# One-hots for the spreading of expert weights: from VectorE alone to GpSimd and VectorE, one turn earlier

## The chip, the cores and the metric

The kernel runs on one core of one Trainium2 chip. The metric is the device time of one execution in microseconds; the kernel before takes 3607.58 us, the median of three runs (3606.92 to 3616.43).

## The reference

Two networks are computed one after the other on 256 tokens of width 1024, in float32. The first has two layers of mixed attention and a dense feed-forward part; the change does not touch it. The second has two layers of attention, each followed by a feed-forward part with 16384 experts of which every token uses few. For a block of tokens, cut to what matters:

```python
q = (hb @ w_q).reshape(n, PEER_HEADS, PEER_QDIM)              # 8 heads
s1, s2 = q1 . sub_keys[0], q2 . sub_keys[1]                   # 128 keys each
v1, i1 = lax.top_k(s1, 16);  v2, i2 = lax.top_k(s2, 16)
top_s, pos = lax.top_k(v1 + v2 for all 16 x 16 pairs, 16)
expert = i1 * 128 + i2 at pos                                 # 8 x 16 = 128 per token
g = jax.nn.softmax(top_s, axis=-1)
act = gelu(sum_d u_tab[expert] * hb)
out = sum_hk (g * act) * v_tab[expert]
```

In layer 0 this is done for the 256 tokens and for 256 tokens of a context; in layer 1 only for the 256 tokens.

## The kernel before, in words

The kernel gathers no rows of the tables. It computes every one of the 128 x 128 experts for every token and multiplies each activation with a weight that is zero where the token did not choose the expert. An expert group e is the 128 experts with the same second index.

`ahead` walks the groups e = 0 to 127 (0 to 125 in layer 1). For each, `hidden` loads 512 KB of the table u, splits it into a high and a low part (`cut_in_two`, then `split`: ScalarE casts, L198, VectorE subtracts, L199; the tile tag "ws" has four buffers, two pairs), multiplies it on TensorE with the tokens in three products (`mac`, L232 to L234; 24 matmuls of 256 columns for 256 tokens, 48 for 512), applies the gelu on ScalarE (L1104) and stores the result in HBM (`kept`). 256 tokens of a group are called a unit here. In layer 0 the context half of the first 39 groups has been stored before, so layer 0 has 39 + 2 x 89 = 217 units and layer 1 has 126. `experts` then reads everything back, multiplies with the weights (tensor G) and with the table v.

While `ahead` runs, side generators are advanced after each unit. A plan (P0 for layer 0, P1 for layer 1) gives each a unit at which it starts and a rate in steps per unit. There are two kinds. `choose` finds a block's 16 best per head on VectorE and ends with R, which holds for every token (column) and every one of its 128 choices (partition) the first index, the second index, and the weight g in two parts. `spread` turns R of one block of 128 tokens into the dense weights of these tokens for all 128 x 128 experts, and writes them to G. Layer 0 has four blocks, two for the tokens and two for the context; layer 1 has two. In P0 the spreads start at units 38, 83, 121 and 169 with rates 0.9, 0.8, 0.9 and 0.95; in P1 at 45 and 85 with rates 0.5 and 0.85, so that the two overlap. In layer 0 a generator that loads rows of ada_w into buffers of the tag "wb" (`ada_rest`, VectorE L766) starts with the last spread.

One step of `spread` handles four tokens, and is called a turn here; a spread has 32. For each token VectorE makes three one-hot matrices of 128 choices by 128 keys in f16, in one tile E of the tag "wb" (three buffers): the first index compared with 0 to 127 (L1056), and the second index compared and multiplied by either part of g (L1058, twice). TensorE multiplies the first, as the stationary operand, with each of the other two (L1061), into a PSUM tile of four tokens; ScalarE copies that to a tile of 16 tokens (L1062), which goes to HBM once full (L1064). The four tokens' matmuls follow the one-hots of the same turn in the program. A planner of the language orders the instructions of each engine and adds the semaphores, so that pieces of a turn can stand between pieces of other work; each engine then runs its instructions in that order.

Of the kernel before, what the change touches and what calls it, by code (L numbers as in the profile page):

```python
# [12 lines left out]
F16 = mybir.dt.float16  # L13
U32 = mybir.dt.uint32
AF = mybir.ActivationFunctionType
ALU = mybir.AluOpType
AX = mybir.AxisListType

P = 128
# [5 lines left out]
NT = 16  # L25
GSCALE = 2.0 ** 14
# [27 lines left out]
class Net:  # L54
# [72 lines left out]
    def more_consts(self):  # L127
        nc, io = self.nc, self.io
        self.iota = self.const("iota", [P, P])
        self.mask_q = self.const("mask_q", [P, P])  # L130
        self.mask_k = self.const("mask_k", [P, P])
        self.mask_c = self.const("mask_c", [P, 2, 15])
        self.valid = self.const("valid", [P, 2])
        self.rope1 = self.const("rope1", [P, 2, 2, 8])
        self.rope2 = self.const("rope2", [P, 2, 2, P])
        self.iota16 = self.cst.tile([P, P], F16, tag="iota16", name="iota16")
        nc.vector.tensor_copy(self.iota16, self.iota)
        self.ones4 = self.cst.tile([4, S], F32, tag="ones4", name="ones4")
        nc.vector.memset(self.ones4, 1.0)
        self.cone = self.cst.tile([P, 1], F32, tag="cone", name="cone")  # L140
        nc.vector.memset(self.cone, 1.0)
# [821 lines left out]
    def choose(self, sd, s):  # L963


        nc = self.nc
        room = self.t(sd.t8, [P, 2048])

        def cut(a, n, k, dtype=F32):
            r = room[:, a:a + n]  # L970
            return (r if dtype is F32 else r.bitcast(dtype)).rearrange("p (h k) -> p h k", k=k)

        v, iu, fi = cut(0, 256, 16), cut(256, 256, 16, U32), cut(512, 128, 16, F16)
        ts, pu = cut(768, 128, 16), cut(896, 128, 16, U32)
        pi, pf = cut(1024, 128, 16, U32), cut(1152, 128, 16)
        sel = room[:, 1280:1664].rearrange("p (c h k) -> p c h k", c=3, k=16)
        gz = room[:, 1664:1672]
        ra, rb = cut(1672, 128, 16), cut(1800, 128, 16)
        for hh in range(16):
            tmp = self.t("k2", [P, P])  # L980
            self.top16(v[:, hh], iu[:, hh], s[:, hh], tmp)
            yield
        nc.vector.tensor_copy(fi, iu)
        cand = self.t(sd.t8, [P, 8, 112])
        v4 = v.rearrange("p (h c) k -> p h c k", c=2)
        for lo, n, a0, m in ((0, 4, 0, 16), (64, 12, 4, 4)):
            nc.vector.tensor_tensor(cand[:, :, lo:lo + n * m].rearrange("p h (a b) -> p h a b", b=m),
                                    v4[:, :, 0, a0:a0 + n, None].to_broadcast([P, 8, n, m]),
                                    v4[:, :, 1, None, 0:m].to_broadcast([P, 8, n, m]), op=ALU.add)
        yield  # L990
        for h in range(8):
            tmp = self.t("k2", [P, 112])
            self.top16(ts[:, h], pu[:, h], cand[:, h], tmp)
            yield

        far = pf
        nc.vector.tensor_copy(far, pu)
        nc.vector.tensor_scalar(far, far, 63.5, None, ALU.is_gt)
        for half in range(2):
            for r, (sh, mask) in ((ra, (4, 15)), (rb, (2, 3))):  # L1000
                if half == 0:
                    nc.vector.tensor_scalar(pi, pu, sh, None, ALU.logical_shift_right)
                else:
                    nc.vector.tensor_scalar(pi, pu, mask, None, ALU.bitwise_and)
                nc.vector.tensor_copy(r, pi)
            yield
            if half == 0:
                nc.vector.tensor_scalar(rb, rb, -12.0, None, ALU.add)
            nc.vector.tensor_sub(rb, rb, ra)
            nc.vector.tensor_mul(rb, rb, far)  # L1010
            nc.vector.tensor_add(ra, ra, rb)
            f4 = fi.rearrange("p (h c) k -> p h c k", c=2)
            yield
            for k in range(0, 16, 8):
                eq = self.t("k2", [P, 8, 8, 16], F16)
                nc.vector.tensor_tensor(eq, ra[:, :, k:k + 8, None].rearrange("p h k r -> p k h r").to_broadcast([P, 8, 8, 16]),
                                        self.iota[:, None, None, 0:16].to_broadcast([P, 8, 8, 16]), op=ALU.is_equal)
                yield
                nc.vector.tensor_mul(eq, eq, f4[:, None, :, half].to_broadcast([P, 8, 8, 16]))
                yield  # L1020
                for n in (8, 4, 2):
                    nc.vector.tensor_add(eq[:, :, :, 0:n], eq[:, :, :, 0:n], eq[:, :, :, n:2 * n])
                nc.vector.tensor_add(sel[:, half, :, k:k + 8].rearrange("p h k -> p k h"), eq[:, :, :, 0], eq[:, :, :, 1])
                yield
        gs = sel[:, 2]
        nc.vector.tensor_sub(gs, ts, ts[:, :, 0:1].to_broadcast([P, 8, 16]))
        nc.scalar.activation(gs, gs, AF.Exp)
        nc.vector.tensor_reduce(gz, gs, AX.X, ALU.add)
        nc.vector.reciprocal(gz, gz)
        nc.vector.tensor_mul(gs, gs, gz[:, :, None].to_broadcast([P, 8, 16]))  # L1030
        pt = self.p(sd.pt, [P, 3, P])
        for j in range(3):
            nc.tensor.transpose(pt[:, j], sel[:, j].rearrange("p h k -> p (h k)"), self.ident)
        R = self.t("R", [P, 4, P], bufs=2)
        g = self.t("k2", [P, P])
        g16 = self.t("k2", [P, P], F16)
        nc.scalar.copy(R[:, 0:2], pt[:, 0:2])
        nc.scalar.activation(g, pt[:, 2], AF.Copy, scale=GSCALE)
        nc.vector.tensor_copy(g16, g)
        nc.vector.tensor_copy(R[:, 2], g16)  # L1040
        nc.vector.tensor_sub(R[:, 3], g, R[:, 2])
        return R

    def spread(self, r, Gd, nb):


        nc = self.nc
        for q in range(P // NT):
            st = self.t("k8", [P, P, NT])
            for m in range(0, NT, 4):  # L1050
                n = q * NT + m
                pG = self.p("C", [P, 4, P])
                E = self.t("wb", [P, 4, 3, P], F16)
                for j in range(4):
                    k0, k1, g0, g1 = (r[:, i, n + j:n + j + 1] for i in range(4))
                    nc.vector.tensor_scalar(E[:, j, 0], self.iota16, k0, None, ALU.is_equal)  # L1056
                    for i, g in enumerate((g0, g1)):
                        nc.vector.tensor_scalar(E[:, j, 1 + i], self.iota16, k1, g, ALU.is_equal, ALU.mult)  # L1058
                for j in range(4):
                    for i in range(2):  # L1060
                        nc.tensor.matmul(pG[:, j], E[:, j, 0], E[:, j, 1 + i], start=i == 0, stop=i == 1)  # L1061
                nc.scalar.activation(st[:, :, m:m + 4], pG.rearrange("p n e -> p e n"), AF.Copy, scale=1 / GSCALE)  # L1062
                if m == NT - 4:
                    nc.sync.dma_start(Gd[:, nb + q], st)  # L1064
                yield

    def routing(self, l, hs, Gd, order, early, plan):

        ss = [self.t("k8", [P, 16, P]) for _ in range(2 * len(hs))]
        R = {}

        def choose(i):
            R[i] = yield from self.choose(self.rt, ss[i])

        def spread(gen, i, nb):
            self.done(gen)
            yield from self.spread(R[i], Gd, nb)

        gens = [choose(i) for i, _ in order]
        for _ in self.key_scores(l, hs, ss):
            for g in gens[:early]:
                next(g), next(g)
        gens += [spread(g, *o) for g, o in zip(gens, order)]
        return [(t, g, r) for g, (t, r) in zip(gens, plan)]
# [324 lines left out]
```

## Time and profile before

| | |
|---|---|
| median of three runs | 3607.58 us (3606.92 to 3616.43) |
| profiled execution | 3616.49 us, span 3614.7 us |
| TensorE matmul busy | 3506.5 us (97%), 22400 matmuls |
| weight load busy | 3053.3 us (84%) |
| VectorE busy | 2563.6 us (71%), 6767 instructions |
| ScalarE busy | 1520.0 us (42%) |
| GpSimd busy | 51.9 us (1%), 72 instructions |
| mean granted TensorE clock | 0.991 of full speed |
| chain of work that ended last | 67% TensorE, 21% VectorE, 8% DMA; L1058 6%, L1056 2%, L199 4% |

The profile is of one execution. Busy time is the time in which at least one instruction of an engine runs; matmuls are pipelined, so they overlap one another, and TensorE can be busy throughout and still do more or less work in a microsecond. The instructions of VectorE overlap a little too: the next starts before the one in front of it has ended, so the distance from start to start is what an instruction takes of the engine.

### The profile page before, as it was taken

The page shows a single profiled execution, that of the slowest core. Times are in us where ns is not written, and L with a number is a line of the kernel's source. Part 1 is how long each engine was busy: PE and PEld are TensorE (multiplying, and loading weights), DVE is VectorE, ACT ScalarE, POOL GpSimd, SP SyncE. Part 2 cuts the span into 40 slices and gives each one's busy share as a digit, 9 for nine tenths or more (in the row PEclk, how much of TensorE's full clock was granted, in tenths as well). Part 3 has the DMA queues.
Part 4 walks back from the last instruction along what each step waited for, and adds up shares of the span by engine and source line. Part 5 has one row for each costly group of instructions (what it writes and reads, how often), then busy time and mean ns, then how long its engine had stood idle before and what let it go on. Part 6 is the DMA issues. An engine that isn't in the chain of part 4 may idle for free.

```text
span 3614.7 us, 59733 instructions
## 1 busy us (share of the span) xinstructions
PE 3506.5 (97%) x22400; PEld 3053.3 (84%) x22400; DVE 2563.6 (71%) x6767; ACT 1520.0 (42%) x2555; POOL 51.9 (1%) x72
## 2 busy tenths in 40 slices
PE   8999989999999999999999999999999999999999
PEld 6677777899899999998997888888878999888877
DVE  6666776655753799999777655554476789987666
ACT  5533455544553433333333222222254545455443
POOL 1000010000000000000000000000000000000000
PEclk9999999999999999999999999999999999999999
DMA  6555644566522754454579877776223677788986
GB/s 220 168 175 199 209 153 131 184 202 201 167 94 82 223 183 166 163 174 175 181 246 295 263 249 237 236 226 188 76 72 110 214 234 239 240 275 293 291 259 197
DMA packets 329394, 712.85 MB, mean 197 GB/s; under 512 B 28304, under 2 KB 170256, under 8 KB 322704
## 3 DMA queue, kind: packets, MB, share of 16 engines
q1 hardware_dynamic: 329104, 709.05, 60.5%
q8 instruction: 175, 2.87, 0.3%
q14 instruction: 115, 0.94, 0.1%
HBM read 606.44 MB, written 102.50 MB: 196 GB/s over the span
## 4 chain that ended last, share of the span: by engine, by line
PE 67%; DVE 21%; DMA 8%; issue 1%; ACT 1%; SPq 1%; POOL 0%; DVEq 0%; POOLq 0%; ACTq 0%
PE psC L233 9%; PE psC L234 9%; PE psC L232 9%; PE psA L234 8%; PE psA L232 8%; PE psA L233 8%; DVE wb L1058 6%; DVE ws L199 4%; DMA wb<-in_v 3%; DMA k<-kept 3%; PE psB L233 3%; PE psB L232 3%; PE psB L234 3%; DVE wb L1056 2%; DVE k L199 2%; DMA wb<-in_ada_w 1%
## 5 line engine op out<-in xcount | busy, mean ns | idle before, releaser
L198 ACT CAST ws<-w 128x1024 fp32r<-128x1024 f32 (+1 forms) x528 | 547.6, 1037 | 923.5 <-PE psA L233 626.1
L199 DVE TENSOR_TENSOR ws<-w,ws 128x1024 fp32r<-128x1024 f32 (+1 forms) x528 | 635.6, 1205 | 366.4 <-ACT ws L198 360.9
L234 PE MATMUL psA<-b,ws 128*128 128x256 f32 x2760 | 784.2, 284 | 29.3 <-DVE ws L199 28.2
L232 PE MATMUL psA<-b,ws 128*128 128x256 f32 x2760 | 787.4, 285 | 1.1 <-ACT ws L198 1.1
L233 PE MATMUL psA<-b,ws 128*128 128x256 f32 x2760 | 776.6, 281 | 0.0
L234 PEld LDWEIGHTS psA<-b,ws 128*128 128x128 f32 x2760 | 521.8, 189 | 43.7 <-DVE ws L199 43.1
L232 PEld LDWEIGHTS psA<-b,ws 128*128 128x128 f32 x2760 | 522.3, 189 | 7.0 <-ACT ws L198 3.6
L233 PEld LDWEIGHTS psA<-b,ws 128*128 128x128 f32 x2760 | 522.6, 189 | 0.2
L234 PE MATMUL psC<-k,k 128*128 128x512 f32 x1056 | 416.3, 395 | 7.0 <-DVE k L199 6.9
L232 PE MATMUL psC<-k,k 128*128 128x512 f32 x1056 | 417.1, 395 | 6.0 <-ACT k L198 6.0
L233 PE MATMUL psC<-k,k 128*128 128x512 f32 x1056 | 416.4, 394 | 0.0
L1058 DVE TENSOR_SCALAR wb<-iota,R 128x128 f16<-128x128 f16 x1536 | 413.3, 307 | 0.0
L199 DVE TENSOR_TENSOR k<-wb,k 128x1024 fp32r<-128x1024 f32 x256 | 312.4, 1220 | 60.8 <-ACT k L198 60.6
L198 ACT CAST k<-wb 128x1024 fp32r<-128x1024 f32 x256 | 268.4, 1050 | 199.4 <-DMA wb<-in_v 199.1
L198 ACT CAST k<-k 128x256 fp32r<-128x256 f32 (+1 forms) x272 | 137.3, 506 | 484.0 <-PE psA L234 422.6
L1151 DVE TENSOR_TENSOR k<-k,b 128x256 f32<-128x256 f32 x384 | 149.9, 421 | 211.7 <-DMA k<-kept 209.7
L234 PEld LDWEIGHTS psC<-k,k 128*128 128x128 f32 x1056 | 198.5, 188 | 60.3 <-DVE k L199 15.0
L233 PE MATMUL psC<-ws,k 128*128 128x512 f32 (+1 forms) x608 | 240.5, 396 | 5.7 <-DVE ws L199 4.6
L232 PEld LDWEIGHTS psC<-k,k 128*128 128x128 f32 x1056 | 198.9, 188 | 52.6 <-ACT k L198 8.1
L232 PE MATMUL psC<-ws,k 128*128 128x512 f32 (+1 forms) x608 | 239.7, 398 | 0.6 <-ACT k L198 0.2
L234 PE MATMUL psC<-ws,k 128*128 128x512 f32 (+1 forms) x608 | 238.0, 392 | 0.0
L233 PEld LDWEIGHTS psC<-k,k 128*128 128x128 f32 x1056 | 199.0, 188 | 44.2
(400 smaller groups left out, 6250.0 us busy)
## 6 DMA issues: line engine op xcount, KB each, us to landing
w<-in_u SPq DMA_DIRECT2D x256, 512.0 KB, 4.3
wb<-in_v SPq DMA_DIRECT2D x256, 512.0 KB, 4.5
w<-in_w_ff SPq DMA_DIRECT2D x128, 512.0 KB, 4.5
G<-k SPq DMA_DIRECT2D x48, 1024.0 KB, 6.1
b<-G SPq DMA_DIRECT2D x48, 1024.0 KB, 8.5
wb<-in_ada_w SPq DMA_DIRECT2D x80, 512.0 KB, 4.7
k<-kept SPq DMA_DIRECT2D x128, 256.0 KB, 3.8
w<-in_wA SPq DMA_DIRECT2D x48, 512.0 KB, 4.7
```

Source lines behind the costliest of these rows:

```text
L198: self.nc.scalar.copy(hi, src)
L199: self.nc.vector.tensor_sub(lo, src, hi.bitcast(F32))
L232: self.nc.tensor.matmul(out, ah, bh, start=first, stop=False)
L233: self.nc.tensor.matmul(out, ah, bl, start=False, stop=False)
L234: self.nc.tensor.matmul(out, al, bh, start=False, stop=last)
L1056: nc.vector.tensor_scalar(E[:, j, 0], self.iota16, k0, None, ALU.is_equal)
L1058: nc.vector.tensor_scalar(E[:, j, 1 + i], self.iota16, k1, g, ALU.is_equal, ALU.mult)
L1151: nc.vector.tensor_mul(g3, g3, Gs[i][:, :, j])
```

## The change

The three one-hots of a turn are made differently, and one turn earlier. The stationary one-hots are made by GpSimd, one `tensor_scalar` for each of the four tokens. The moving ones are made by VectorE for four tokens at once, with three `tensor_tensor` of 512 elements: a comparison, and two multiplications of its result with the two parts of g. Two tokens lie interleaved, so that the innermost dimension of these operands has two elements, those of two neighbouring tokens; the matmul reads the moving operand with a step of two elements. For this a copy of 0 to 127 with each number twice is made once (`iota2`), and R is held in f16 except for the first index (R0). A step makes the one-hots of the next turn and then issues the matmuls of the present one; a spread has 33 steps, the first of which makes one-hots alone. The plans, the rates, the buffers and all other code are unchanged.

```diff
+        self.iota2 = self.cst.tile([P, P, 2], F16, tag="iota2", name="iota2")
+        nc.vector.tensor_copy(self.iota2, self.iota[:, :, None].to_broadcast([P, P, 2]))
...
-        R = self.t("R", [P, 4, P], bufs=2)
+        R, R0 = self.t("R", [P, 3, P], F16, bufs=2), self.t("R0", [P, P], bufs=2)
         g = self.t("k2", [P, P])
-        g16 = self.t("k2", [P, P], F16)
-        nc.scalar.copy(R[:, 0:2], pt[:, 0:2])
+        nc.scalar.copy(R0, pt[:, 0])
+        nc.scalar.copy(R[:, 0], pt[:, 1])
         nc.scalar.activation(g, pt[:, 2], AF.Copy, scale=GSCALE)
-        nc.vector.tensor_copy(g16, g)
-        nc.vector.tensor_copy(R[:, 2], g16)
-        nc.vector.tensor_sub(R[:, 3], g, R[:, 2])
-        return R
+        nc.vector.tensor_copy(R[:, 1], g)
+        nc.vector.tensor_sub(R[:, 2], g, R[:, 1])
+        return R, R0
...
-        for q in range(P // NT):
-            st = self.t("k8", [P, P, NT])
-            for m in range(0, NT, 4):
-                n = q * NT + m
-                pG = self.p("C", [P, 4, P])
-                E = self.t("wb", [P, 4, 3, P], F16)
-                for j in range(4):
-                    k0, k1, g0, g1 = (r[:, i, n + j:n + j + 1] for i in range(4))
-                    nc.vector.tensor_scalar(E[:, j, 0], self.iota16, k0, None, ALU.is_equal)
-                    for i, g in enumerate((g0, g1)):
-                        nc.vector.tensor_scalar(E[:, j, 1 + i], self.iota16, k1, g, ALU.is_equal, ALU.mult)
-                for j in range(4):
-                    for i in range(2):
-                        nc.tensor.matmul(pG[:, j], E[:, j, 0], E[:, j, 1 + i], start=i == 0, stop=i == 1)
-                nc.scalar.activation(st[:, :, m:m + 4], pG.rearrange("p n e -> p e n"), AF.Copy, scale=1 / GSCALE)
-                if m == NT - 4:
-                    nc.sync.dma_start(Gd[:, nb + q], st)
-                yield
+        st, (r, r0) = None, r
+
+        def ones(n):
+            E = self.t("wb", [P, 4, 512], F16)
+            first = E[:, 0].rearrange("p (j e) -> p j e", e=P)
+            for j in range(4):
+                nc.gpsimd.tensor_scalar(first[:, j], self.iota16, r0[:, n + j:n + j + 1], None, ALU.is_equal)
+            pairs = [E[:, 1 + i].rearrange("p (h e j) -> p h e j", h=2, j=2) for i in range(3)]
+            for i in range(3):
+                col = r[:, i, n:n + 4].rearrange("p (h j) -> p h j", j=2)[:, :, None].to_broadcast([P, 2, P, 2])
+                nc.vector.tensor_tensor(pairs[i], pairs[0] if i else self.iota2[:, None].to_broadcast([P, 2, P, 2]), col,
+                                        op=ALU.mult if i else ALU.is_equal)
+            return first, pairs
+
+        E = ones(0)
+        yield
+        for n in range(0, P, 4):
+            q, m = divmod(n, NT)
+            nxt = ones(n + 4) if n + 4 < P else None
+            if m == 0:
+                st = self.t("k8", [P, P, NT])
+            pG = self.p("C", [P, 4, P])
+            for j in range(4):
+                for i in range(2):
+                    nc.tensor.matmul(pG[:, j], E[0][:, j], E[1][1 + i][:, j // 2, :, j % 2], start=i == 0, stop=i == 1)
+            nc.scalar.activation(st[:, :, m:m + 4], pG.rearrange("p n e -> p e n"), AF.Copy, scale=1 / GSCALE)
+            if m == NT - 4:
+                nc.sync.dma_start(Gd[:, nb + q], st)
+            E = nxt
+            yield
```

## Rows read from the trace of the kernel before

**Rows 1.** Busy time by engine: window, length, then busy us and instructions of each engine.

```profile
1280.00:1880.00 600.00, 571.43 (x5127) 553.21 (x5126) 556.63 (x2344) 210.80 (x321) 0.00 (x0) 0.99 0.54 182
2920.00:3230.00 310.00, 300.44 (x2662) 288.06 (x2662) 296.88 (x1061) 154.90 (x250) 0.00 (x0) 1.00 0.74 246
```

**Rows 2.** The same for instructions on tile psA: first PE, PEld, then DVE, ACT.

```profile
1200.00:1240.00 40.00, 40.00 (x341) 39.84 (x340) 0.00 (x0) 5.26 (x14) 1.00 0.74 234
1280.00:1880.00 600.00, 516.47 (x4092) 495.17 (x4091) 0.00 (x0) 50.56 (x86) 0.99 0.54 182
2920.00:3230.00 310.00, 276.23 (x2145) 259.63 (x2145) 0.00 (x0) 33.53 (x89) 1.00 0.74 246
```

**Rows 3.** The same for line L1061, the small matmuls: PE and PEld.

```profile
1280.00:1880.00 600.00, 80.54 (x1024) 59.70 (x1024) 0.99 0.54 182
2920.00:3230.00 310.00, 44.56 (x512) 30.43 (x512) 1.00 0.74 246
```

**Rows 4.** Chain that ended last, 1250 to 2060: start us, length us, piece.

```profile
1851.70 0.91 PE psC L1061 x16
```

**Rows 5.** The same chain, 3120 to 3160: shares by line, and one split.

```profile
by line: DVE wb L1058 48.3%; DVE ws L199 28.3%; DVE wb L1056 16.4%; PE psA L234 3.1%; PE psA L232 2.1%; PE psA L233 2.0%; issue 0.1%; DVEq L199 0.1%
...
3121.20 1.13 DVE ws L199
```

**Rows 6.** Waits from 1280 to 1880: us in total, times, longest us.

```profile
ACT ws L198 <- PE psA L233: 269.2, 64, 7.8
...
PE psA L234 <- DVE ws L199: 20.9, 30, 2.3
...
DVE b L766 <- DMA wb<-in_ada_w: 9.1, 5, 3.7
...
PE psC L1061 <- DVE wb L1058: 5.2, 19, 1.2
```

**Rows 7.** Timeline of VectorE, 3140 to 3152: start us, us, instruction.

```profile
3142.55 0.25 DVE L1056 TENSOR_SCALAR wb<-iota,R 128x128 f16<-128x128 f16 x1
...
3143.16 0.25 DVE L1056 TENSOR_SCALAR wb<-iota,R 128x128 f16<-128x128 f16 x1
...
3144.99 0.24 DVE L1056 TENSOR_SCALAR wb<-iota,R 128x128 f16<-128x128 f16 x1
```

**Rows 8.** VectorE's groups, 1280 to 1880: busy us, mean ns, idle before.

```profile
L1016 DVE TENSOR_TENSOR k<-k,c_iota 128x1024 f16<-128x1024 f32 x12 | 14.6, 1216 | 0.0
...
L1019 DVE TENSOR_TENSOR k<-k,k 128x1024 f16<-128x1024 f16 x12 | 8.2, 684 | 0.0
...
L1022 DVE TENSOR_TENSOR k<-k 128x512 f16<-128x512 f16 x12 | 5.0, 417 | 0.0
```

**Rows 9.** Timeline of VectorE, 1388 to 1404.

```profile
1394.92 0.41 DVE L1022 TENSOR_TENSOR k<-k 128x512 f16<-128x512 f16 x1
1395.25 0.30 DVE L1058 TENSOR_SCALAR wb<-iota,R 128x128 f16<-128x128 f16 x1
```

**Rows 10.** Groups of GpSimd and one of VectorE, whole span.

```profile
L151 POOL TENSOR_TENSOR rsrb<-rsvb,neghalf 128x4 f32<-128x4 f32 x4 | 4.0, 1008 | 111.5 <-DVE rsvb L150 111.5
L151 POOL TENSOR_TENSOR rsrb<-rsvb,neghalf 128x1 f32<-128x1 f32 x6 | 3.4, 573 | 29.6 <-DVE rsvb L150 29.6
...
L381 POOL MEMSET k<- 128x3 f32 x16 | 1.5, 103 | 56.7 <-DVE k L386 54.3 <-PE psA L420 1.8 <-ACT k L387 0.3
...
L842 DVE TENSOR_TENSOR k<-k,k 128x512 f32<-128x512 f32 x8 | 5.4, 680 | 0.0
```

**Rows 11.** Timeline of VectorE and GpSimd at two places.

```profile
458.80 1.23 DVE L199 TENSOR_TENSOR ws<-w,ws 128x1024 fp32r<-128x1024 f32 x1
458.81 1.63 POOL L151 TENSOR_TENSOR rsrf<-rsvf,neghalf 128x1 f32<-128x1 f32 x1 [59.79 <-DVE rsvf L150]
...
979.46 1.01 POOL L151 TENSOR_TENSOR rsrf<-rsvf,neghalf 128x4 f32<-128x4 f32 x1 [0.39 <-DVE rsvf L150]
979.55 0.68 DVE L842 TENSOR_TENSOR k<-k,k 128x512 f32<-128x512 f32 x1
```

## The prediction

> **What bounds the kernel now.** I read the stretches of the span first (busy time of each engine by window), then the same windows for single tiles and lines, then the waits and the chain of work that ended last in the worst window, and last the VectorE and GpSimd rows. `spread` runs in two stretches: A, 1280 to 1880 us, four spreads of 32 turns in layer 0 (1024 small matmuls of L1061), and B, 2920 to 3230 us, two spreads in layer 1 (512) [rows 1, 3]. A turn is four tokens, 8 small matmuls; there are 128 turns in A and 64 in B.
>
> TensorE looks full in both (571 of 600, 300 of 310 us), but a busy matmul is not a matmul at its peak. In the stretch without a spread, 1200 to 1240, 341 expert matmuls fit in 40.0 us, 0.1173 us each [rows 2]; 16 small ones run in 0.91 us, 0.057 each [rows 4]. So the work in A is 4092 x 0.1173 + 1024 x 0.057 = 480.0 + 58.4 = 538.4 us in 600, and in B 2145 x 0.1173 + 512 x 0.057 = 251.6 + 29.2 = 280.8 in 310 [rows 2, 3]. What TensorE loses is 61.6 us in A and 29.2 in B, 90.8 together. Outside these stretches the change does nearly nothing, so about 91 us is the most that it can give.
>
> Who takes that time: VectorE is busy 556.6 of 600 and 296.9 of 310 [rows 1]. From 3120 to 3160 the chain lies on it to over nine tenths, 65% on the one-hots (L1056, L1058), 28% on the split of the weights (L199) [rows 5]. The wait that ends last for TensorE in A is that of the expert matmul L234 for this split, 20.9 us in 30 waits, against 5.2 for the one-hots themselves [rows 6]: the one-hots delay TensorE mostly by standing ahead of the split in VectorE's queue.
>
> **The change part by part.** *Removed:* 12 tensor_scalar a turn on VectorE. From the L1056 of one token to that of the next is 0.61 us (3142.55 to 3143.16), and four tokens take 2.44 (to 3144.99) [rows 7]: 128 x 2.44 = 312 us in A, 64 x 2.44 = 156 in B.
>
> *Added on VectorE:* 3 tensor_tensor a turn over 512 f16 elements. The nearest row is L1022, 512 f16, 417 ns; L1019 with 1024 f16 takes 684 and L1016 with 1024 f32 inputs 1216 [rows 8], so f16 operands run here at about two elements a cycle, and a 16-element inner run repeated over a middle dimension (L1019) keeps that. From one L1022 to the next instruction is 0.33 us (1394.92 to 1395.25) [rows 9]. A turn is 3 x 0.33 + about 0.09 for the two multiplications that wait for the comparison's result (0.42 less 0.33) = 1.08 us. Not shown is an inner run of only two elements, one 4-byte pair of columns repeated 128 times. Bounds: 0.33 us as above, or 0.60 at L1016's rate for half its elements (1216/2, the fixed part counted as start-up). I take 0.33: the operands are f16 with step one, as in L1019. So VectorE's load falls to 556.6 - 312 + 138 = 383 us in A and 296.9 - 156 + 69 = 210 in B.
>
> *Moved to GpSimd:* 4 tensor_scalar of 128 f16 a turn, 512 in A and 256 in B; GpSimd does nothing there now [rows 1]. The trace has no such instruction. Below stands a MEMSET of 3 columns, 103 ns; above the power of L151, 573 ns for one column and 1008 for four [rows 10], 0.43 us fixed and 0.145 a column, which for 128 columns would be 19 us. A comparison isn't a power, so I set the column near VectorE's f32 rate (1216 ns for 1024, 1.2 ns, 0.15 us for 128 [rows 8]) and get 0.25 with the MEMSET's fixed part and 0.58 with the power's; I take 0.45, nearer the power, since both read operands. A turn is 1.8 us of GpSimd; at full TensorE speed a turn comes every 538.4/128 = 4.2 us in A and every 24 x 0.1173 + 8 x 0.057 = 3.27 us in the worst part of B, where there is one turn to an expert (four tokens between two splits [rows 7]). It keeps up. Nothing is queued behind GpSimd but the next one-hots; TensorE's small matmuls wait for it, and they get a turn of lead.
>
> *VectorE and GpSimd at one port:* a power of one column that started at 458.81, with the two-input split of VectorE from 458.80, took 1.63 us instead of 0.57: it stood until the split was over. The other way, the two-input L842 (128x512) at 979.55 took its usual 0.68 though GpSimd worked from 979.46 to 980.47 [rows 10, 11]; but that power reads only four columns. So GpSimd surely waits for VectorE; what VectorE waits for GpSimd lies between 0 and the whole 0.45 an instruction: 0 to 230 us in A, 0 to 115 in B. I take the reading of 128 columns, 0.15: 77 and 38. VectorE then stands at 460 in A and 248 in B, below TensorE's 538 and 281. Where the chain lay on VectorE at 3120, a turn was 1.13 + 2.44 = 3.57 us and becomes 1.13 + 1.08 + 0.60 = 2.81, below TensorE's 3.27. [...]
>
> *At nothing:* the matmuls now read every second f16, 4 bytes a column; the expert matmuls read 4-byte columns at 256 in 0.117 us already [rows 2], so 0.057 stays. The extra iota copy and the split evacuation of R are a handful of instructions, once in the kernel or once in a spread, beside TensorE's work. The evacuation L1062 and the G store keep their number. The turn ahead keeps two E tiles of three "wb" buffers in use, three where two spreads overlap (the end of B): VectorE and GpSimd then write a buffer that TensorE read one turn before instead of three, so they can't run ahead. One step more per spread (33 instead of 32) ends it a unit later, before the last expert.
>
> *The sum.* Of 61.6 and 29.2 us not all returns: 9.1 us of VectorE's idle time in A are waits for ada_w loads [rows 6], short bursts remain where selection and spreading meet, and the buffers couple the engines. I take 60%: 37 + 18 = 55 us. The profiled execution was 3616.5 us (span 3614.7), which gives 3561.5; it stands 8.9 us above the median of the three runs, 3607.6, so the forecast is 3607.6 - 55 = 3553 us.
>
> **Rivals.**
> 1. *The port costs more than it frees (slower).* Place: the same two stretches. VectorE plus waiting passes today's length when each GpSimd instruction shuts it out for more than (600 - 383)/512 = 0.42 us in A and (310 - 210)/256 = 0.39 in B. At 0.45: 383 + 230 = 613, +13; 210 + 115 = 325, +15; with GpSimd's own lateness at the small matmuls some more, 3640 us. For it: 458.81, and nearly all that VectorE still does in B has two SBUF inputs. Against: L842. The same end is reached if GpSimd is slow in itself: above 3.27/4 = 0.82 us an instruction with its waits, TensorE waits for it at the end of B, above 1.05 in A. Together 0.24.
> 2. *The repeated pair of columns runs at one element a cycle.* Then a turn is 3 x 0.60 + 0.09 = 1.9 us, VectorE stands at 383 + 105 + 77 = 565 in A and 210 + 52 + 38 = 300 in B; at most 35 + 10 us are left to win, of which 60% are 27: 3581. For it: no row has an inner run of two. Against: L1016 reads one f32 element 16 times over and still takes 1216. Chance 0.14. [...]
> 3. *All of the loss returns:* 3607.6 - 91 = 3517; needs GpSimd's waits hidden everywhere. 0.10.
> 4. *No change:* VectorE is freed, but the split still comes late, since ScalarE's cast ahead of it waits for buffers (ACT for psA L233, 269 us in A [rows 6]), or the spread's matmuls now wait for GpSimd instead. 3607; 0.10. Against: with VectorE free the split follows its cast at once, as from 1200 to 1240, where nothing is lost.
>
> **How the numbers follow.** Forecast 0.42, rivals 0.24, 0.14, 0.10, 0.10. Faster: 0.42 + 0.14 + 0.10 = 0.66; the same (within 0.3%, 11 us, about what a measurement can tell) 0.10; slower 0.24. The range reaches from near rival 3, 3520, to rival 1's 3640; beyond lie about 0.06 below and 0.12 above. The forecast's own range is 3535 to 3575 (80 to 36% of the loss back).
>
> **What would show it.** Right: VectorE's tensor_tensor of 512 near 0.42 us, its busy time in A and B down by a quarter or more, GpSimd instructions of 0.3 to 0.6 us, the wait of L234 for L199 nearly gone, expert matmuls at 0.117 us through the spreads, both stretches shorter by about 37 and 18 us. Wrong: GpSimd busy nearly throughout, L199 far above 1.22 us or starting late after GpSimd, small matmuls that wait for GpSimd, or tensor_tensor at 0.69 us.

## The result and the profile after

The changed kernel takes 3569.52 us in the median of four runs (3565.71 to 3571.16), against 3607.25 before; the ratio is 0.9889, 95% interval 0.987 to 0.9907. It is 38 us faster. The forecast was 3553, 55 us faster; the measured time lies inside the forecast's range.

The page of the changed kernel, first part and the costliest group that is new (columns: instructions and mean ns, then idle time before them and what ended it):

```profile
PE 3469.8 (97%) x22400; PEld 3036.8 (85%) x22400; DVE 2333.5 (65%) x5034; ACT 1518.0 (43%) x2561; POOL 746.0 (21%) x840
...
L1055 POOL TENSOR_SCALAR wb<-iota,R 128x128 f16<-128x128 f16 x768 | 694.2, 921 | 541.8 <-ACT R L1038 402.6
```

VectorE lost 230 us of busy time and GpSimd took on 694: its instruction lasts 0.92 us in the mean, where 0.45 was forecast. Line numbers have shifted: L199 of before is L201, L232 to L234 are L234 to L236, and L1061 is L1073.

What this did to the two layers shows between the first and the last store of `kept` in each. These times are read from the timeline of the queue that issues the stores (SyncE): before, layer 0 took 731.1 us (1175.5 to 1906.7) and layer 1 412.5; after, 690.9 and 411.4. So 40 us came out of layer 0, where 37 were forecast, and 1 out of layer 1, where 18 were. (The profiled executions differ by 51 us, more than the medians: the one of before was 9 us above its median, the one of after 4 below. The surplus lies outside the two layers.)

The stretches of the changed kernel, busy time by engine (PE, PEld, DVE, ACT, POOL, then clock and DMA), for two typical windows, one of layer 0 and one near the end of layer 1:

```profile
1600.00:1640.00 40.00, 40.00 (x381) 39.72 (x380) 34.77 (x133) 15.92 (x24) 38.06 (x46) 1.00 0.53 189
...
3080.00:3120.00 40.00, 32.84 (x303) 30.10 (x303) 23.97 (x45) 17.86 (x30) 40.00 (x49) 1.00 0.66 231
```

The same two windows for the expert matmuls (tile psA) alone:

```profile
1600.00:1640.00 40.00, 35.98 (x293) 34.88 (x292) 0.00 (x0) 3.55 (x6) 1.00 0.53 189
...
3080.00:3120.00 40.00, 26.33 (x207) 24.89 (x207) 0.00 (x0) 3.39 (x9) 1.00 0.66 231
```

At 1600, 293 expert matmuls and 88 small ones are 293 x 0.1173 + 88 x 0.057 = 39.4 us of work in 40: TensorE loses almost nothing beside a spread at full rate. At 3080 it does 207 x 0.1173 + 96 x 0.057 = 29.8 us of work in 40, GpSimd is busy for all of the 40, and VectorE has 16 us to spare. Where before the chain lay on VectorE [rows 5], the bound is now GpSimd. These 40 us hold 12 turns (96 small matmuls) but only 8.6 experts (207 expert matmuls, 24 an expert): where the two spreads of layer 1 overlap there are about 1.4 turns to an expert, as the plan's rates, 0.5 and 0.85, say.

The waits of layer 1's spreads, 2880 to 3190, changed kernel: the weight loads of the small matmuls wait for GpSimd (us in total, times, longest):

```profile
PEld L1073 <- POOL wb L1055: 23.0, 32, 1.7
```

In layer 0, 1270 to 1840, the wait of the expert matmul for VectorE's split (20.9 us before [rows 6]) has shrunk to this:

```profile
PE psA L236 <- DVE ws L201: 0.2, 1, 0.2
```

In layer 1's spreads no such wait is listed: there the small matmuls now wait for GpSimd instead.

How the two engines slow each other shows in the timeline of the changed kernel, GpSimd first, then VectorE at the same place:

```profile
1517.28 0.59 POOL L1055 TENSOR_SCALAR wb<-iota,R 128x128 f16<-128x128 f16 x1
...
1518.17 2.40 POOL L1055 TENSOR_SCALAR wb<-iota,R 128x128 f16<-128x128 f16 x2 [0.29 <-POOL wb L1055]
```

```profile
1518.12 0.42 DVE L1059 TENSOR_TENSOR wb<-iota,R 128x512 f16<-128x512 f16 x1 [3.02 <-PE psC L1073]
1518.53 1.32 DVE L201 TENSOR_TENSOR ws<-w,ws 128x1024 fp32r<-128x1024 f32 x1
```

VectorE waited idly until 1518.12, and the GpSimd instruction at 1517.28 took 0.59 us. The next two begin beside a tensor_tensor and the split, and take 2.40 us together. Over all 768, sorted by how much of their length lies beside a VectorE instruction with two SBUF inputs: those with none have a median of 0.597 us and follow one another at 0.578; those that lie beside one for over nine tenths (245) have a median of 1.26. In 12 places a GpSimd instruction begins during a split after which VectorE pauses for over 0.8 us; in all 12 it ends 0.47 us after the split, so that it stood until the split was nearly over, given its 0.6 us alone. VectorE loses much less: in the place above the split takes 1.32 us instead of 1.22.

### The profile page after: what moved, and what is told of

The parts are those of the page before. It is cut to its first block, busy times and chain, and to the rows that moved or that the text cites. A ratio compares the mean times of both kernels' runs of the same rounds, so it can differ in the third digit from the quotient of the medians.

```text
span 3563.6 us, 59207 instructions
## 1 busy us (share of the span) xinstructions
PE 3469.8 (97%) x22400; PEld 3036.8 (85%) x22400; DVE 2333.5 (65%) x5034; ACT 1518.0 (43%) x2561; POOL 746.0 (21%) x840
## 5 line engine op out<-in xcount | busy, mean ns | idle before, releaser
L201 DVE TENSOR_TENSOR ws<-w,ws 128x1024 fp32r<-128x1024 f32 (+1 forms) x528 | 641.1, 1215 | 414.1 <-ACT ws L200 410.3
L1055 POOL TENSOR_SCALAR wb<-iota,R 128x128 f16<-128x128 f16 x768 | 694.2, 921 | 541.8 <-ACT R L1038 402.6
L234 PE MATMUL psA<-b,ws 128*128 128x256 f32 x2760 | 786.2, 285 | 0.0
L236 PE MATMUL psA<-b,ws 128*128 128x256 f32 x2760 | 777.0, 282 | 1.0 <-DVE ws L201 0.5
L236 PEld LDWEIGHTS psA<-b,ws 128*128 128x128 f32 x2760 | 520.5, 189 | 3.1 <-DVE ws L201 2.8
L234 PEld LDWEIGHTS psA<-b,ws 128*128 128x128 f32 x2760 | 520.9, 189 | 0.4 <-ACT k L1117 0.3
L236 PE MATMUL psC<-k,k 128*128 128x512 f32 x1056 | 416.9, 395 | 6.4 <-DVE k L201 6.3
L234 PE MATMUL psC<-k,k 128*128 128x512 f32 x1056 | 416.8, 395 | 5.3 <-ACT k L200 5.2
L153 POOL TENSOR_TENSOR rsrf<-rsvf,neghalf 128x1 f32<-128x1 f32 (+5 forms) x38 | 41.4, 1094 | 1620.4 <-DVE rsvf L152 1620.4
L201 DVE TENSOR_TENSOR k<-wb,k 128x1024 fp32r<-128x1024 f32 x256 | 312.7, 1222 | 61.0 <-ACT k L200 60.6
L236 PEld LDWEIGHTS psC<-k,k 128*128 128x128 f32 x1056 | 198.8, 188 | 59.4 <-DVE k L201 14.7
L234 PEld LDWEIGHTS psC<-k,k 128*128 128x128 f32 x1056 | 198.7, 188 | 51.8 <-ACT k L200 8.1
L234 PE MATMUL psC<-ws,k 128*128 128x512 f32 (+1 forms) x608 | 239.4, 398 | 1.1 <-ACT ws L200 0.6
L236 PE MATMUL psC<-ws,k 128*128 128x512 f32 (+1 forms) x608 | 238.0, 392 | 0.0
```

The costliest lines, as they stand in the source:

```text
L153: nc.gpsimd.tensor_tensor(r[:m, :cols], v[:m, :cols], self.neghalf[:m, :cols], op=ALU.pow)
L201: self.nc.vector.tensor_sub(lo, src, hi.bitcast(F32))
L234: self.nc.tensor.matmul(out, ah, bh, start=first, stop=False)
L236: self.nc.tensor.matmul(out, al, bh, start=False, stop=last)
L1055: nc.gpsimd.tensor_scalar(first[:, j], self.iota16, r0[:, n + j:n + j + 1], None, ALU.is_equal)
```

## The experiments

Each is an edit of the changed kernel unless it says otherwise; in the order in which they stand they are called e1 to e8. Code cuts are shortened. Ratios are to the kernel before on the same chip (3611.89 us beside e1 to e4, 3611.7 beside e5 to e8, 3607.25 beside the changed kernel), so it is the ratios that compare best. "Layer 0" and "layer 1" are the times from the first to the last store of `kept` in the profile of each, as above.

### Stationary one-hots back on VectorE

```diff
-                nc.gpsimd.tensor_scalar(first[:, j], self.iota16, r0[:, n + j:n + j + 1], None, ALU.is_equal)
+                nc.vector.tensor_scalar(first[:, j], self.iota16, r0[:, n + j:n + j + 1], None, ALU.is_equal)
```

> The changed kernel with the stationary one-hots back on VectorE (four tensor_scalar a turn); the three tensor_tensor and the turn of lead stay. Theory 1, GpSimd's rate: what the change did not win is the stretch at the end of layer 1 where two spreads overlap and GpSimd, at 0.81 us an instruction, is busy without a gap; VectorE then needs 1.13 + 1.2 + 4 x 0.165 = 3.0 us a turn there, under TensorE's 3.27, so the stretch from first to last kept store in layer 1 shrinks from 411 to about 392 us, that of layer 0 stays at 691, and the time is near 3550. Theory 2, the port: GpSimd also slows VectorE everywhere, so L201 goes from 1.23 back to 1.22 us in the mean and layer 0 shrinks too, by 5 us or more. Theory 3, VectorE is still the bound: the 0.66 us a turn that it takes back cost 192 x 0.66 = 127 us of its time, and the kernel is slower than the changed one, 3580 or more.

3549.74 us, ratio 0.9824 (0.9808 to 0.9841): faster than the changed kernel, with GpSimd taken out. Layer 1 takes 389.8 us, as theory 1 had it; theory 3 falls. Layer 0 takes 686.1 instead of 690.9, which is theory 2's sign or GpSimd's rate in layer 0 (from 1720 to 1760 in the changed kernel GpSimd is busy for all of the 40 us and TensorE for 37.06); the mean of L201 is 1.222 us against 1.231 over the whole kernel, so that GpSimd beside it slows 512 splits by some 5 us together and leaves most of the 22 us in layer 1 to GpSimd's lateness.

### A fourth tensor_tensor, no GpSimd

```diff
-            first = E[:, 0].rearrange("p (j e) -> p j e", e=P)
-            for j in range(4):
-                nc.gpsimd.tensor_scalar(...)
-            pairs = [E[:, 1 + i].rearrange("p (h e j) -> p h e j", h=2, j=2) for i in range(3)]
+            pairs = [E[:, i].rearrange("p (h e j) -> p h e j", h=2, j=2) for i in range(4)]
...
-                    nc.tensor.matmul(pG[:, j], E[0][:, j], E[1][1 + i][:, j // 2, :, j % 2], ...)
+                    nc.tensor.matmul(pG[:, j], E[0][:, j // 2, :, j % 2], E[2 + i][:, j // 2, :, j % 2], ...)
```

R holds all of its four rows in f16 here.

> No GpSimd: the stationary one-hots come from a fourth tensor_tensor of 512 on VectorE, interleaved as the others, so that the weight load reads every second f16. VectorE needs about 1.6 us a turn. Theory 1 (GpSimd's rate): as e1 or slightly faster, near 3548, layer 1 at about 392 us. Rival: a weight load with a step of two is slower; at the 0.189 us of the f32 loads instead of 0.096 the eight loads of a turn cost 0.7 us more, 192 x 0.7 = 140 us of TensorE, and the time is over 3600.

3543.56 us, ratio 0.9812 (0.9796 to 0.9829), layer 0 683.4 and layer 1 388.7. This is among the fastest versions; its ratio is 0.008 below that of the changed kernel, about 28 us. The rival did not come: the weight load of the one-hots, group by form in this kernel and then in the changed one, takes the same with a step of two elements as with a step of one:

```profile
L1069 PEld LDWEIGHTS <-wb 128*128 128x128 f16 x1536 | 88.5, 97 | 5.5
```

```profile
L1073 PEld LDWEIGHTS <-wb 128*128 128x128 f16 x1536 | 88.7, 96 | 5.8 <-issue 0.2
```

VectorE's tensor_tensor over 2880 to 3170 us of this kernel, and over 2880 to 3190 of the changed one beside GpSimd (mean ns after the comma):

```profile
L201 DVE TENSOR_TENSOR ws<-w,ws 128x1024 fp32r<-128x1024 f32 x87 | 106.1, 1220 | 23.3 <-ACT ws L200 23.3
L1055 DVE TENSOR_TENSOR wb<-iota,R 128x512 f16<-128x512 f16 x128 | 49.7, 419 | 28.2 <-PE psC L1069 28.2
L1055 DVE TENSOR_TENSOR wb<-wb,R 128x512 f16<-128x512 f16 x128 | 48.6, 417 | 0.1
```

```profile
L201 DVE TENSOR_TENSOR ws<-w,ws 128x1024 fp32r<-128x1024 f32 x88 | 109.8, 1247 | 28.7 <-ACT ws L200 28.2
L1059 DVE TENSOR_TENSOR wb<-wb,R 128x512 f16<-128x512 f16 x128 | 53.7, 450 | 0.4
L1059 DVE TENSOR_TENSOR wb<-iota,R 128x512 f16<-128x512 f16 x64 | 27.5, 431 | 56.6 <-PE psC L1073 54.3 <-POOL wb L1055 2.2
```

This is what GpSimd beside it costs VectorE: 27 ns on a split, 12 to 33 on a one-hot, 88 x 0.027 + 128 x 0.033 + 64 x 0.012 = 7 us in layer 1's 310, spent while it has time to spare.

### Half of the stationary one-hots on GpSimd

```diff
-                nc.gpsimd.tensor_scalar(...)
+                (nc.gpsimd if j % 2 else nc.vector).tensor_scalar(...)
```

> The changed kernel with two of the four stationary one-hots of a turn on GpSimd and two on VectorE. Theory 1 (rate): GpSimd needs 2 x 0.81 = 1.6 us a turn and is never the bound, VectorE 1.13 + 1.2 + 0.33 = 2.7 at the end of layer 1: layer 1 shrinks to about 392 us, the time is near 3550. Theory 2 (port): half of the slowing of VectorE remains; between the changed kernel and e1.

3544.95 us, ratio 0.9821 (0.9805 to 0.9837), layer 0 683.3, layer 1 388.1: all of what e1 and e2 gained, with GpSimd still in use. Two windows near the end of layer 1; the second is to be held against the one of the changed kernel above, and the first has most of the overlap of the two spreads, which end earlier here:

```profile
3040.00:3080.00 40.00, 40.00 (x404) 39.55 (x402) 37.03 (x91) 23.13 (x39) 33.95 (x33) 1.00 0.84 287
3080.00:3120.00 40.00, 40.00 (x389) 39.62 (x387) 35.37 (x82) 22.01 (x38) 29.96 (x28) 1.00 0.83 290
```

In the first, 33.95 us for 33 GpSimd instructions are 1.03 us each, more than in the changed kernel, but with two a turn TensorE does not wait. The number of GpSimd instructions a turn decides; the slowing of VectorE beside GpSimd does not (theory 2 had this run lie between the changed kernel and e1).

### The two spreads of layer 1 apart

```diff
-P1 = ((5, 0.75), (41, 1.0), (45, 0.5), (85, 0.85))
+P1 = ((5, 0.75), (41, 1.0), (45, 0.9), (85, 0.85))
```

> The changed kernel with the first spread of layer 1 at rate 0.9 instead of 0.5, so that it ends (unit 82) before the second begins (85). GpSimd still makes all stationary one-hots. Theory 1 (rate): a turn then comes every 24 x 0.1173 / 0.9 + 0.46 = 3.6 us, over GpSimd's 4 x 0.81 = 3.2, so TensorE no longer waits for it: layer 1 shrinks from 411 to about 395, the time to about 3553. Theory 2 (port) and theory 3 (VectorE): nothing changes for them but the order, 3570 within 8 us; with selection and spread together VectorE may even be fuller, then 3575.

3564.23 us, ratio 0.9875 (0.9859 to 0.9892), whose interval overlaps that of the changed kernel. Layer 0 takes 691.7 us, as in the changed kernel. Layer 1 takes 396.3 us, as theory 1 had it (395): with GpSimd's work unchanged and only spread out, the wait goes, and TensorE is full in the window that held the loss:

```profile
3080.00:3120.00 40.00, 40.00 (x381) 39.57 (x381) 27.64 (x43) 21.39 (x35) 34.81 (x43) 1.00 0.81 272
```

The total moved by 5 us instead of 15. From the last store of `kept` to the end the profile of this run took 388.8 us, that of the changed kernel 380.5, those of e1 to e3 384.5 to 386.4, that of before 381.7. This does not follow the length of layer 1: e5 below has a layer 1 of 412.8 us and takes 387.0 from there to the end, e7 has 389.9 and takes 382.7. Part of it is TensorE's clock: over that stretch the granted clock was 0.99 in this run and 1.00 in the changed kernel, an estimated 4 us of work. The rest is open; the four runs of this kernel go from 3560.0 to 3571.6. So the layer's time bears theory 1 out, and the total, 11 us above its 3553, does not.

### Without the turn of lead

```diff
-        E = ones(0)
-        yield
         for n in range(0, P, 4):
             q, m = divmod(n, NT)
-            nxt = ones(n + 4) if n + 4 < P else None
+            E = ones(n)
...
-            E = nxt
             yield
```

> The changed kernel without the turn of lead: a step makes its own one-hots, GpSimd still the stationary ones, VectorE three tensor_tensor; a spread has 32 steps again. Theory 1 (load and rate: the gain is VectorE's relief, the rest is GpSimd's rate): GpSimd waits for buffers alone and can run ahead by itself, so little changes, 3570 within 12 us. Theory 4, the lead: the gain needs the lead, because TensorE would wait for GpSimd's four instructions (4 x 0.6 to 0.8 = 2.4 to 3.2 us) in a good part of the 192 turns; then at least half of the gain goes, 3590 or more.

3574.04 us, ratio 0.989 (0.9872 to 0.9908): no difference from the changed kernel. Layer 0 takes 693.8, layer 1 412.8, in a profiled execution 11 us above the median, whose granted clock in layer 1 was 0.98 (1.00 in the changed kernel). GpSimd runs ahead by itself: in the first spread its four one-hots of a turn are done 4.2 us (median) before the first small matmul of that turn, 4.5 in the changed kernel.

### The lead alone, on the kernel before

```diff
+        E = ones(0)
+        yield
...
+            nxt = ones(n + 4) if n + 4 < P else None
...
+            E = nxt
```

Here `ones` holds the twelve tensor_scalar of before.

> The kernel before with nothing but the turn of lead: twelve tensor_scalar a turn on VectorE as before, made one step ahead of their matmuls. Theory 1: VectorE's load is unchanged and full, so nothing is won, 3608 within 10 us. Theory 4 (lead): TensorE's waits for the one-hots, 15 us in all, and what follows from them go, 3590 or less.

3625.60 us, ratio 1.0036 (1.0024 to 1.0047): a loss of 13 us against the kernel before on that chip, which is outside theory 1's 10 and on the other side of theory 4. Layer 0 takes 744.9 us against 731.1. Waits of this kernel from 1280 to 1890:

```profile
PE psA L234 <- DVE ws L199: 21.8, 27, 2.3
...
DVE wb L1054 <- PE psC L1069: 15.0, 12, 2.6
```

The wait for the split is as before [rows 6], but VectorE now waits 15.0 us for TensorE to free a one-hot buffer (6.6 in the same stretch of before), since two of the three are held. With VectorE as full as before [rows 1], that is time it can hardly make up. Most of the 14 us by which layer 0 is longer shows in TensorE's clock. Three stretches of the kernel before, just ahead of a fall of the granted clock, in it, and behind it:

```profile
1473.00:1477.00 4.00, 1.73 (x23) 1.51 (x23) 4.00 (x21) 2.50 (x4) 0.00 (x0) 1.00 0.44 178
1477.00:1480.50 3.50, 3.50 (x18) 3.50 (x18) 3.50 (x18) 0.00 (x0) 0.00 (x0) 0.51 0.92 317
1480.50:1484.00 3.50, 3.50 (x32) 3.45 (x32) 3.50 (x17) 0.08 (x1) 0.00 (x0) 1.00 0.47 143
```

TensorE stood idle for 2.3 of 4 us, VectorE was busy throughout; then the granted clock was 0.51 of full speed instead of 1.00, and 18 matmuls were done in the time of 32. The stretches at half of full speed add up to 10 us in layer 0 of the kernel before (from 1477, 1624 and 1655 us, 3.4 us each), to 31 in e6 and to nothing in the changed kernel. As an estimate, half of that is lost: 5, 15 and 0 us. By this estimate 10 of e6's 14 us in this layer are clock; whether the medians' 13 us divide in the same way is not shown.

### The fourth tensor_tensor without the lead

The same edit as for e5, on e2.

> e2 (four tensor_tensor on VectorE, no GpSimd) without the turn of lead. Theory 1: VectorE has room, so the one-hots are ready anyway, 3544 to 3555. Theory 4: as far as the lead matters it shows here without GpSimd, 3560 or more.

3545.74 us, ratio 0.9813 (0.9796 to 0.983), layer 0 683.0, layer 1 389.9: equal to e2. With or without GpSimd, the lead gives nothing once VectorE has room.

### Half of the columns on GpSimd

```diff
-                nc.gpsimd.tensor_scalar(first[:, j], self.iota16, r0[:, n + j:n + j + 1], None, ALU.is_equal)
+                nc.gpsimd.tensor_scalar(first[:, j, 0:64], self.iota16[:, 0:64], r0[:, n + j:n + j + 1], None, ALU.is_equal)
+                nc.vector.tensor_scalar(first[:, j, 64:P], self.iota16[:, 64:P], r0[:, n + j:n + j + 1], None, ALU.is_equal)
```

> The changed kernel with columns 0 to 63 of each stationary one-hot from GpSimd and 64 to 127 from VectorE (tensor_scalar). It sizes GpSimd's instruction: 0.578 us from start to start for 128 columns when VectorE leaves it alone. If it is mostly fixed cost, as my prediction's 0.30 + 0.15 had it, 64 columns take 0.43 us or more; if it is mostly columns, about 0.35 or less. In time: theory 1 lets the wait at the end of layer 1 go when four of them with their waits for VectorE fit in 3.27 us, so layer 1 shrinks from 411 to 390 to 400 and the time to 3550 to 3560; but VectorE gives back 192 x 0.66 = 127 us of its time as in e1.

3566.80 us, ratio 0.9876 (0.9859 to 0.9893). Undisturbed, an instruction of 64 columns takes 0.437 us and is followed by the next after 0.413, against 0.597 and 0.578 for 128: by a line through these two sizes 0.25 us fixed and 2.6 ns a column, between the two expectations. Layer 0 took 692.4, layer 1 406.3, outside the 390 to 400 of theory 1. If GpSimd's own work were what fills its time there, 4 x 0.165 us less in each of some 30 turns would have given 20 us. It gave 5. The instructions got shorter and their waits longer, as the next window shows. The window, for comparison with e3's second:

```profile
3080.00:3120.00 40.00, 36.49 (x347) 34.83 (x346) 32.97 (x99) 19.90 (x33) 39.44 (x51) 1.00 0.72 243
```

39.44 us for 51 instructions are 0.77 us each, at 0.41 us of own work: 0.36 us, nearly half, is waiting for VectorE, which is fuller here than in the changed kernel (40.00 us for 49 there: 0.82 each, 0.24 of it waiting). So theory 1 has to be put more exactly: what counts here is the number of times that GpSimd has to get in between VectorE's instructions, not the columns that it then works on.

## Why the prediction was right, and where not

- *The ceiling.* TensorE's work at 0.1173 and 0.057 us was the right floor: in the windows where nothing waits (1600 to 1640 above) 39.4 of 40 us are filled by it. The best versions take 683 and 388 us for the layers, 48 and 24 under before, 72 of the 91 us.
- *VectorE's three tensor_tensor.* Forecast near 0.42 us each, which is L1022's row [rows 8]; measured 0.417 to 0.419 without GpSimd, 0.431 to 0.450 beside it. Rival 2, with 0.60 us each for the pair of columns, is out: the repeated pair takes 0.417 us, as in L1022's row. No run shows the length of a cycle, in which the prediction counts; what [rows 8] give, as an estimate, is 0.52 ns for one more f16 element (684 less 417 over 512) and 1.04 for one of f32 (1216, less the same fixed 150, over 1024), two to one.
- *VectorE's relief is the gain.* Shown for layer 0, where 40 us came back (forecast 37), the wait of the expert matmul for the split fell from 20.9 to 0.2 us, and the lead, which could have been the cause instead, gives nothing (e5, e7) or costs (e6). That wait is about half of the 40 us. Another 5 us, by the estimate at e6, are the clock, which fell three times in this layer before and for which the prediction's sum has no term. The rest is not split up.
- *The step that failed: GpSimd's term.* The prediction set its instruction at 0.45 us and said "It keeps up" with a turn every 3.27 us at the end of layer 1, with 0.82 us as the point at which it would not. Two things were wrong in that. First, the instruction: undisturbed it is 0.58 us, and beside VectorE it was 12.92 us for 16, 0.81 each, 3.2 us a turn. The prediction had read from 458.81 that GpSimd "surely waits for VectorE", but gave that wait no price in its 1.8 us a turn. Second, the turn: it took one turn to an expert, and there are about 1.4 where the spreads overlap. (In its own window of before, eight tokens' one-hots, two turns, stand between the splits at 3141.41 and 3147.43.) At full speed the 29.8 us of TensorE's work at 3080 make 12 turns, one every 2.5 us, so that the point lies at 0.62 us an instruction. By this estimate GpSimd would just have kept up at 0.58; with its waits it does not. Changed kernel, timeline of GpSimd, 3080 to 3092:

```profile
3079.32 12.92 POOL L1055 TENSOR_SCALAR wb<-iota,R 128x128 f16<-128x128 f16 x16
```

  So the 18 us of layer 1 stayed away. That it is GpSimd's rate, waits included, with the two spreads together, and not VectorE or the lead, is shown by e3 (half the instructions, layer 1 is 24 us under before) and e4 (all the instructions, spread out, 16 us under before). It is rival 1's second clause, in one stretch only; the rest of that rival, a loss, did not come.
- *The port.* The prediction priced one direction only, VectorE's, at 0.15 us for each GpSimd instruction. Measured is 7 us in layer 1 for 256 of them, 0.03 each. GpSimd pays instead: 0.58 us become 0.8 in the mean at 3080, and 1.26 in the median of those beside two-input work. That one engine stands for nearly a whole instruction of the other is seen in GpSimd's direction (1518.17 and 458.81 [rows 11]) and not in VectorE's, where a whole instruction would have been 0.6 us. No run shows a port, or what else the two share: the word, here and in theory 2, is the author's explanation, and measured is only how much each slows the other.
- *The 60% share* was 65% in layer 0 and 4% in layer 1. The share was taken, not worked out, so that the first came near it is partly luck. Layer 0 has some of the second's loss too: e2 and e3 take 7 us less than the changed kernel there. One such place is the last spread, 1720 to 1760, where GpSimd is busy throughout; VectorE's work on the ada_w rows runs there too.

## What to carry to other kernels

Moving work to an idle engine needs that engine's rate, in the stretch where most of it is wanted: the mean share of 21% here hides a window of 100%, and a plan that lets two producers overlap adds up their demands on what they share. Take the rate with the waits for other engines in it: undisturbed, GpSimd's would just have sufficed here. When an engine is relieved, look first at whether fewer and longer instructions on the same engine do (four tensor_tensor in place of twelve tensor_scalar, 64 to 68 us won without GpSimd), and only then at another engine. Check a lead in time by taking it away: here it gave nothing, as the queue ran ahead by itself (4.2 us in e5), and on the kernel before it cost 13 us.

## What the runs showed of the hardware

A GpSimd tensor_scalar on f16 with a scalar for each partition took 0.413 us from start to start for 64 columns (e8) and 0.578 for 128 (changed kernel); a line through the two gives an estimated 0.25 us fixed and 2.6 ns a column. Beside VectorE's two-input instructions one of 128 columns took 1.26 us in the median instead of 0.597, and one that began during a split stood almost to its end (it ended 0.47 us after the split, in 12 of 12 places), while VectorE's split and one-hots were lengthened by only 0.01 to 0.03 us in the mean. A tensor_tensor on f16 with an inner run of two and a repeated pair took 0.417 to 0.419 us for 512 elements (e2), as L1022's did (0.417 [rows 8]). Matmuls on f16 operands with a step of two elements ran nearly as those with a step of one: 0.058 us from start to start with the moving operand so read (changed kernel) against 0.056 (before), and 0.097 us for the load of the weights (e2) against 0.096 (changed kernel). In the kernel before the granted clock fell to 0.51 of full speed after TensorE had stood idle for 2.3 of 4 us, and 18 matmuls were then done in the time of 32.
